# One-hot tiles of the gates: two tokens innermost instead of four

## The chip, the cores and the metric

The kernel runs on one core of one Trainium2 chip. The metric is the device time of one execution in microseconds. Before the change it is 1978.94 us, the median of three runs (1978.42 to 1980.65).

## The reference

The model has two layers over 256 tokens of width 1024. Layer 0 mixes with a gated linear attention beside an RWKV-7 scan, layer 1 with sparse attention. Behind each mixer stands a feed-forward part that picks 128 of 16384 experts for every token (8 heads of 16). The change lies in this part alone:

```python
q = (x @ w_q).reshape(B, T, PEER_HEADS, 2, PEER_DKEY // 2)
s = jnp.einsum('bthcd,hcnd->bthcn', q, sub_keys)
top_s, top_i = lax.top_k(s, PEER_TOPK)
cand_s = (top_s[..., 0, :, None] + top_s[..., 1, None, :]).reshape(B, T, PEER_HEADS, -1)
cand_i = (top_i[..., 0, :, None] * PEER_NKEYS + top_i[..., 1, None, :]).reshape(...)
best_s, pos = lax.top_k(cand_s, PEER_TOPK)
idx = jnp.take_along_axis(cand_i, pos, axis=-1)
gate = jax.nn.softmax(best_s, axis=-1)
h = gelu(einsum('md,mkd->mk', xb, exp_u[ib]))
coef = gate * h
out = einsum('mk,mkd->md', coef, exp_v[ib])
```

An expert's number is a pair of keys (a, b), each below 128, and its number is 128 a + b.

## The kernel before

The kernel gathers no experts. In `peer` it multiplies all tokens with all 16384 rows of u, 128 rows to a tile (128 tiles, L255 to L276, the u loop), and later with all rows of v (L283 to L308, the v loop). Between the two, every coefficient is multiplied by its gate, which is zero for experts that were not picked. The coefficients stand in two SBUF tiles, `Ca` and `Cb`: partition = second key, then the first key (72 of them in `Ca`, 56 in `Cb`), then the token.

A weight tile is read by one DMA of 512 KB on SP's queue (L86). ScalarE rounds it to a high part `wh` (L100), VectorE subtracts to get the low part `wl` (L101), and TensorE does three products of 256 columns for each of eight slices (L112 to L114 in the u loop, 24 matmuls a tile) or of 512 columns (L122 in the v loop, 12 matmuls a tile). ScalarE puts the Gelu of two u tiles into `Ca` or `Cb` (L264, L267).

The picks of a token come from `route`, which runs on VectorE during the first part of the u loop. It leaves the tile `picks`: 128 picks on the partitions, and for each of 256 tokens the first key, the second key and the gate as two f16 numbers (high and low part).

From this `gates` builds the gate matrix of four tokens at a time, 64 groups in a layer. `B` (`ohB`) is the one-hot code of the second key, `A` (`ohA`) that of the first key, multiplied by the two parts of the gate. Both come from a comparison of `iota` (0 to 127, every number repeated for each token) with `picks` (L318, L319), and `A` from two products in place (L321). Then TensorE adds, for each of the four tokens, two products of 128 columns: `B` of the token is the stationary operand, `A` of the token the moving one (L324, 8 matmuls a group). VectorE multiplies the result in PSUM into the coefficients that are already there (L330); where the u loop has not been yet, ScalarE copies it (L332) and the Gelu is multiplied in later (L268).

What sets the order: `peer` runs u tiles and pulls steps of the background work (`route`, then `gates`) by a budget of 1.65 a tile, a group of gates costing 2.1 (L246 to L276). A tile framework adds the waits, and it lets an instruction on an engine go ahead of others of the code where its operands are there early: the one-hots of the first groups run at 308 us, long before the first gate matmul. Behind that, one-hots are built about one group ahead of their matmuls. The pools that matter: `ohA` and `ohB` have two buffers each, `wh`, `wl` and `raw` three.

Of the kernel before, what the change touches and what calls it, by code (L numbers as in the profile page):

```python
# [15 lines left out]
F16 = mybir.dt.float16  # L16
AF = mybir.ActivationFunctionType
OP = mybir.AluOpType
# [3 lines left out]
P = 128  # L22
# [47 lines left out]
class Core:  # L70
# [63 lines left out]
    def consts(self):  # L134
        nc, a = self.nc, self.a
        c = self.const.tile([P, 3 * P + 16], F32, name="cst")
        nc.sync.dma_start(c, a["cst"])
        self.ident = c[:, 0:P]
        self.iota = self.const.tile([P, P, 4], F16, name="iota")
        nc.gpsimd.tensor_copy(self.iota, c[:, P:2 * P].unsqueeze(2).to_broadcast([P, P, 4]))  # L140
        self.ones = c[:, 2 * P:3 * P]
        self.iota16 = self.const.tile([P, 16, 16], BF16, name="iota16")
        nc.gpsimd.tensor_copy(self.iota16, c[:, 3 * P:3 * P + 16].unsqueeze(2).to_broadcast([P, 16, 16]))
        e = self.const.tile([P, 2], F32, name="eps")
        nc.vector.memset(e[:, 0:1], LN_EPS)
        nc.vector.memset(e[:, 1:2], LNX_EPS)
        self.eps = e
# [163 lines left out]
    def gates(self, pk, Ca, Cb, picks, t4, k):  # L311
        nc = self.nc
        V = nc.vector
        p = self.aps()
        B = pk.tile([P, P, 4], F16, name="ohB", bufs=2)
        A = pk.tile([P, 2, P, 4], F16, name="ohA", bufs=2)
        bc = lambda n: picks[:, n, t4:t4 + 4].unsqueeze(1).to_broadcast([P, P, 4])
        V.tensor_tensor(B, self.iota, bc(1), op=OP.is_equal)  # L318
        V.tensor_tensor(A[:, 1], self.iota, bc(0), op=OP.is_equal)  # L319
        for m in range(2):  # L320
            V.tensor_mul(A[:, m], A[:, 1], bc(2 + m))  # L321
        for n in range(4):
            for m in range(2):
                nc.tensor.matmul(p[:, n * P:(n + 1) * P], B[:, :, n], A[:, m, :, n], start=m == 0, stop=m == 1)  # L324
        g = p.rearrange("p (t i) -> p i t", t=4)
        for c, o, n in ((Ca, 0, CUT), (Cb, CUT, P - CUT)):
            c = c[:, :, t4:t4 + 4]
            q = min(max(k - o, 0), n)
            if q:
                V.scalar_tensor_tensor(c[:, :q], g[:, o:o + q], 1 / GATE, c[:, :q], op0=OP.mult, op1=OP.mult)  # L330
            if q < n:
                nc.scalar.activation(c[:, q:], g[:, o + q:o + n], AF.Copy, scale=1 / GATE)  # L332
# [677 lines left out]
    def blocks(self, pp, LbT, Tn, Tt):  # L1010
        nc = self.nc
        V, S = nc.vector, nc.scalar
        B, W = 16, P * (P + 1)
        DU = pp.tile([P, 2, B * B], F32, name="DU", tag="ths")
        D, U = (DU[:, n].rearrange("p (m j) -> p m j", m=B) for n in range(2))
        R = pp.tile([P, B * B], F32, name="R", tag="x4", bufs=4)
        nc.gpsimd.memset(U, 0.0)
# [124 lines left out]
```

## Time and profile before

| | |
|---|---|
| median of three runs | 1978.94 us |
| span of the profiled execution | 1976.5 us (the page gives this span as its only time; 2.4 us less than the median) |
| busy: TensorE matmul / VectorE / ScalarE | 97% / 71% / 47% of the span |
| first and last gate matmul, layer 0 | 376.0 and 667.0 us |
| first and last gate matmul, layer 1 | 1307.6 and 1598.7 us |
| gate matmuls (L324) | 1024, each with a weight load of its own |
| one-hot operations of VectorE (L318, L319, L321) | 512 |

Times are from the start of the span. The duration that the profile gives for a matmul or a weight load holds the latency of its pipeline, and neighbours overlap. What a matmul costs when many stand behind one another is read from the distance of their starts, or from the chain of waits, which cuts the time into pieces that don't overlap.

### The profile page before, as it was taken

The numbers are of one execution on the slowest core, as the hardware profiler recorded it, in microseconds if no ns is written. First come the engines' busy times: TensorE is split into PE (matmuls) and PEld (weight loads), VectorE is DVE, ScalarE is ACT, GpSimd is POOL, SyncE is SP. The second block draws the span as 40 slices with busy tenths as digits, with TensorE's granted clock in tenths as the row PEclk, the third lists the DMA queues.
The fourth block names the chain that finished last, engine by engine and source line by source line (L and its number), as shares of the span: only waits on it lengthen the run. The fifth ranks groups of instructions, "written<-read, shape, count | busy, mean of one in ns | idle before, by whom it ended". The sixth has DMA issues, their size and how long they took to land.

```text
span 1976.5 us, 32655 instructions
## 1 busy us (share of the span) xinstructions
PE 1926.1 (97%) x12834; PEld 1759.3 (89%) x12834; DVE 1404.4 (71%) x2860; ACT 932.7 (47%) x1385; POOL 20.8 (1%) x30
## 2 busy tenths in 40 slices
PE   8899899999999999999999989999999999999998
PEld 7898899999999988888888889999999998888886
DVE  6766599877788755556657959977788865555664
ACT  5435355544444444445534745544444444444552
POOL 1000000000000000000001100000000000000000
PEclk9999999999999999999999999999999999999999
DMA  7604345544444566667744445454444456666772
GB/s 225 187 33 130 117 150 161 175 146 148 141 149 146 159 191 191 192 192 232 230 151 150 128 136 173 151 162 148 148 142 147 141 170 192 192 192 195 234 230 76
DMA packets 96313, 323.83 MB, mean 164 GB/s; under 512 B 13984, under 2 KB 19360, under 8 KB 95264
## 3 DMA queue, kind: packets, MB, share of 16 engines
q1 hardware_dynamic: 96160, 321.76, 52.5%
q8 instruction: 100, 1.64, 0.3%
q14 instruction: 53, 0.43, 0.1%
HBM read 318.44 MB, written 3.28 MB: 163 GB/s over the span
## 4 chain that ended last, share of the span: by engine, by line
PE 80%; DVE 12%; DMA 5%; ACT 2%; issue 1%; SPq 0%; DVEq 0%; POOL 0%; ACTq 0%; POOLq 0%
PE acc L122 32%; PE wps L113 11%; PE wps L114 11%; PE wps L112 11%; PE acc L324 6%; DVE wl L101 4%; DMA raw<-v 4%; ACT wh L100 1%; PE acc L112 1%; PE acc L113 1%; PE acc L114 1%; DVE Cb L352 1%; PE wps L548 1%; PE wps L659 1%; PE wps L163 1%
## 5 line engine op out<-in xcount | busy, mean ns | idle before, releaser
L101 DVE TENSOR_TENSOR wl<-raw,wh 128x1024 fp32r<-128x1024 f32 x554 | 677.1, 1223 | 288.8 <-ACT wh L100 284.9
L100 ACT CAST wh<-raw 128x1024 fp32r<-128x1024 f32 x554 | 581.2, 1050 | 613.5 <-PE wps L113 266.3
L112 PE MATMUL wps<-xh,wh 128*128 128x256 f32 x2176 | 630.6, 290 | 0.3 <-ACT wh L100 0.2
L114 PE MATMUL wps<-xh,wl 128*128 128x256 f32 x2176 | 618.0, 284 | 9.9 <-DVE wl L101 9.9
L113 PE MATMUL wps<-xl,wh 128*128 128x256 f32 x2176 | 618.2, 284 | 0.0
L114 PEld LDWEIGHTS wps<-xh,wl 128*128 128x128 f32 x2176 | 419.7, 193 | 11.2 <-DVE wl L101 11.2
L112 PEld LDWEIGHTS wps<-xh,wh 128*128 128x128 f32 x2176 | 422.2, 194 | 1.5 <-ACT wh L100 0.7
L113 PEld LDWEIGHTS wps<-xl,wh 128*128 128x128 f32 x2176 | 420.7, 193 | 0.5 <-DVE xl L168 0.4
L122 PE MATMUL acc<-wh,cl 128*128 128x512 f32 x960 | 298.9, 393 | 0.0
L122 PE MATMUL acc<-wl,ch 128*128 128x512 f32 x960 | 298.1, 392 | 0.8 <-DVE wl L101 0.6
L122 PE MATMUL acc<-wh,ch 128*128 128x512 f32 x960 | 296.8, 390 | 0.0
L122 PEld LDWEIGHTS acc<-wh,ch 128*128 128x128 f32 x960 | 180.1, 188 | 40.9
L122 PEld LDWEIGHTS acc<-wl,ch 128*128 128x128 f32 x960 | 179.8, 188 | 41.0 <-DVE wl L101 3.2
L122 PEld LDWEIGHTS acc<-wh,cl 128*128 128x128 f32 x960 | 180.3, 188 | 39.0
L324 PE MATMUL acc<-ohA,ohB 128*128 128x128 f16 x1024 | 142.6, 296 | 0.0
L330 DVE SCALAR_TENSOR_TENSOR Ca<-acc,Ca 128x288 f32<-128x288 f32 (+12 forms) x128 | 55.2, 432 | 81.8 <-PE acc L324 81.4
L321 DVE TENSOR_TENSOR ohA<-ohA,picks 128x512 f16<-128x512 f16 x256 | 108.0, 422 | 5.4
L324 PEld LDWEIGHTS <-ohB 128*128 128x128 f16 x1024 | 103.8, 118 | 6.9
L112 PE MATMUL acc<-xh,wh 128*128 128x256 f32 x328 | 98.2, 300 | 2.4 <-ACT wh L100 2.4
L113 PE MATMUL acc<-xl,wh 128*128 128x256 f32 x328 | 95.0, 290 | 0.0
L114 PE MATMUL acc<-xh,wl 128*128 128x256 f32 x328 | 93.8, 288 | 0.8 <-DVE wl L101 0.8
L303 ACT CAST ch<-Ca 128x512 fp32r<-128x512 f32 x72 | 44.6, 622 | 83.8 <-PE acc L122 83.8
(397 smaller groups left out, 1747.4 us busy)
## 6 DMA issues: line engine op xcount, KB each, us to landing
raw<-u SPq DMA_DIRECT2D x256, 512.0 KB, 3.6
raw<-v SPq DMA_DIRECT2D x256, 512.0 KB, 4.2
raw<-win SPq DMA_DIRECT2D x41, 512.0 KB, 4.1
raw<-wout SPq DMA_DIRECT2D x16, 512.0 KB, 3.6
raw<-wq SPq DMA_DIRECT2D x16, 512.0 KB, 3.7
gb<-ln SPq DMA_DIRECT2D x2, 1024.0 KB, 5.9
Ca<-subk SPq DMA_DIRECT2D x2, 1024.0 KB, 4.9
Cb<-ln SPq DMA_DIRECT2D x2, 1024.0 KB, 6.8
```

What stands on the lines that cost most here:

```text
L100: self.nc.scalar.copy(h, raw)
L101: self.nc.vector.tensor_sub(l, raw, h.bitcast(F32))
L112: mm(out, h[:, s], xh[:, k], start=k == 0, stop=False)
L113: mm(out, h[:, s], xl[:, k], start=False, stop=False)
L114: mm(out, l[:, s], xh[:, k], start=False, stop=k == 7)
L122: mm(acc[tb * 2 + dh], x[:, c], y[:, dh * 512:(dh + 1) * 512], start=first and n == 0, stop=last and n == 2)
L163: nc.tensor.transpose(p[:, k * P:(k + 1) * P], self.x[:, tb, (g * 4 + k) * P:(g * 4 + k + 1) * P], self.ident)
L303: nc.scalar.copy(ch, C(i))
L321: V.tensor_mul(A[:, m], A[:, 1], bc(2 + m))
L324: nc.tensor.matmul(p[:, n * P:(n + 1) * P], B[:, :, n], A[:, m, :, n], start=m == 0, stop=m == 1)
L330: V.scalar_tensor_tensor(c[:, :q], g[:, o:o + q], 1 / GATE, c[:, :q], op0=OP.mult, op1=OP.mult)
L352: V.match_replace(s[:, g], tv[:, g, 0:8], s[:, g], MARK)
```

## The change

The tiles `ohB`, `ohA` and `iota` get another order in memory. Before, the innermost four elements are the same key of four tokens; a token's column is read with a step of four elements (8 bytes). Now the four tokens are two pairs, each pair has a block of 128 keys x 2 tokens of its own, and a token's column is read with a step of two elements (4 bytes). `iota` holds every number twice instead of four times, and both blocks read it. The operand of `picks` was four neighbouring elements repeated 128 times; now it is two neighbouring elements repeated 128 times, then the next two.

Every operation of VectorE has 512 elements a partition as before, every matmul 128 columns as before. The sequence of instructions and their waits is the same on every engine; only the copy that fills `iota` on GpSimd (L140) has 256 elements instead of 512. One line is added, so lines from L319 on stand one lower in the new kernel.

```diff
-        self.iota = self.const.tile([P, P, 4], F16, name="iota")
-        nc.gpsimd.tensor_copy(self.iota, c[:, P:2 * P].unsqueeze(2).to_broadcast([P, P, 4]))
+        self.iota = self.const.tile([P, P, 2], F16, name="iota")
+        nc.gpsimd.tensor_copy(self.iota, c[:, P:2 * P].unsqueeze(2).to_broadcast([P, P, 2]))
...
-        B = pk.tile([P, P, 4], F16, name="ohB", bufs=2)
-        A = pk.tile([P, 2, P, 4], F16, name="ohA", bufs=2)
-        bc = lambda n: picks[:, n, t4:t4 + 4].unsqueeze(1).to_broadcast([P, P, 4])
-        V.tensor_tensor(B, self.iota, bc(1), op=OP.is_equal)
-        V.tensor_tensor(A[:, 1], self.iota, bc(0), op=OP.is_equal)
+        B = pk.tile([P, 2, P, 2], F16, name="ohB", bufs=2)
+        A = pk.tile([P, 2, 2, P, 2], F16, name="ohA", bufs=2)
+        bc = lambda n: picks[:, n, t4:t4 + 4].rearrange("p (a b) -> p a b", a=2).unsqueeze(2).to_broadcast([P, 2, P, 2])
+        iota = self.iota.unsqueeze(1).to_broadcast([P, 2, P, 2])
+        V.tensor_tensor(B, iota, bc(1), op=OP.is_equal)
+        V.tensor_tensor(A[:, 1], iota, bc(0), op=OP.is_equal)
         for m in range(2):
             V.tensor_mul(A[:, m], A[:, 1], bc(2 + m))
         for n in range(4):
             for m in range(2):
-                nc.tensor.matmul(p[:, n * P:(n + 1) * P], B[:, :, n], A[:, m, :, n], start=m == 0, stop=m == 1)
+                nc.tensor.matmul(p[:, n * P:(n + 1) * P], B[:, n // 2, :, n % 2], A[:, m, n // 2, :, n % 2], start=m == 0, stop=m == 1)
```

## Rows read from the trace of the kernel before

**Rows 1.** The page: busy us, share of the span, instructions of each engine.
```profile
PE 1926.1 (97%) x12834; PEld 1759.3 (89%) x12834; DVE 1404.4 (71%) x2860; ACT 932.7 (47%) x1385; POOL 20.8 (1%) x30
```
**Rows 2.** The page: the chain that ended last, by engine.
```profile
PE 80%; DVE 12%; DMA 5%; ACT 2%; issue 1%; SPq 0%; DVEq 0%; POOL 0%; ACTq 0%; POOLq 0%
```
**Rows 3.** Stretches of the span: both gate stages, then the v loop.
```profile
core 0: us, PE busy (x) PEld busy (x) DVE busy (x) ACT busy (x) POOL busy (x), PEclk, DMA share, GB/s
376.00:667.00 291.00, 291.00 (x2433) 287.50 (x2432) 229.01 (x468) 127.86 (x247) 0.00 (x0) 1.00 0.47 146
1307.60:1598.70 291.10, 291.10 (x2434) 287.57 (x2433) 228.99 (x469) 127.91 (x247) 0.00 (x0) 1.00 0.48 146
667.00:1015.00 348.00, 347.69 (x1587) 287.57 (x1586) 208.78 (x203) 175.96 (x204) 0.00 (x0) 1.00 0.66 205
```
**Rows 4.** Chain of waits, layer 0's gate stage: by line, and a piece (start, us).
```profile
by line: PE wps L113 26.4%; PE wps L112 26.4%; PE wps L114 26.3%; PE acc L324 21.0%
...
441.27 0.96 PE acc L324 x8
```
**Rows 5.** Chain of waits elsewhere: a piece of the v loop, one of layer 0's mixer.
```profile
684.62 252.25 PE acc L122 x1102
134.41 0.75 PE wps L691 x13
```
**Rows 6.** Costliest groups of layer 0's gate stage: count, busy us, mean ns, idle before.
```profile
L112 PE MATMUL wps<-xh,wh 128*128 128x256 f32 x640 | 186.5, 291 | 0.0
L324 PE MATMUL acc<-ohA,ohB 128*128 128x128 f16 x511 | 71.2, 296 | 0.0
```
**Rows 7.** Weight loads by line: duration ns min/median/max, first and last start us, forms.
```profile
L324 PEld LDWEIGHTS <-ohB x1024: 111/117/138, 376.0 to 1598.6; 128*128 128x128 f16 x171
L112 PEld LDWEIGHTS wps<-xh,wh x2176: 186/192/338, 216.5 to 1615.6; 128*128 128x128 f32 x198
L691 PEld LDWEIGHTS wps<-Tn,Lb x32: 133/138/138, 134.0 to 137.9; 128*64 128x64 f32 x32
```
**Rows 8.** One-hot operations by line, same columns.
```profile
L318 DVE TENSOR_TENSOR ohB<-iota,picks x128: 412/416/427, 307.9 to 1591.7; 128x512 f16<-128x512 f16 x128
L319 DVE TENSOR_TENSOR ohA<-iota,picks x128: 415/418/426, 308.4 to 1592.9; 128x512 f16<-128x512 f16 x128
L321 DVE TENSOR_TENSOR ohA<-ohA,picks x256: 405/424/431, 308.9 to 1595.8; 128x512 f16<-128x512 f16 x128
```
**Rows 9.** Waits in layer 0's gate stage: us in total, times, longest us.
```profile
DVE Ca L330 <- PE acc L324: 39.1, 50, 1.6
...
DVE ohB L318 <- PE acc L324: 10.8, 11, 1.6
DVE wl L101 <- ACT wh L100: 7.5, 12, 0.8
```
**Rows 10.** Groups of VectorE outside the stage, shapes kept apart.
```profile
L1026 DVE TENSOR_TENSOR R<-DU 128x225 f32<-128x225 f32 x1 | 0.6, 550 | 0.0
...
L1026 DVE TENSOR_TENSOR R<-DU 128x144 f32<-128x144 f32 x1 | 0.4, 409 | 0.0
L999 DVE TENSOR_TENSOR wk<-wk,dcst 128x256 f32<-128x256 f32 x1 | 0.4, 425 | 0.0
L999 DVE TENSOR_TENSOR wk<-wk,dcst 128x128 f32<-128x128 f32 x1 | 0.3, 285 | 0.0
```
**Rows 11.** Further lines, by line.
```profile
L416 DVE TENSOR_TENSOR Cb<-Ca x2: 272/273/274, 284.6 to 1213.5; 128x128 f32<-128x128 f32 x2
L304 DVE TENSOR_TENSOR cl<-Cb,ch x52: 683/686/694, 877.1 to 1947.3; 128x512 fp32r<-128x512 f32 x52
L140 POOL CAST iota<-cst x1: 609/609/609, 4.2 to 4.2; 128x512 f16<-128x512 f32 x1
```

## The prediction

> **What bounds the kernel now.** I read the page's engine table first, then its chain, then the two stretches in which the gate matmuls run, and last the rows of single operations. The table shows TensorE busy for 97% of the span [rows 1]; since matmul durations overlap, this alone proves little. The chain, which has no overlaps, puts 80% of the span on TensorE and 12% on VectorE [rows 2]. [...] VectorE is early, not late: it waits for the gate matmuls for 39.1 us in front of L330 and 10.8 us in front of L318 [rows 9]. So a nanosecond taken from a gate matmul is a nanosecond of the stage, and one added to a one-hot operation is at first free.
>
> **What a gate matmul costs now.** 21.0% of 291 us is 61.1 us for 64 groups of 8: 119.3 ns each (one piece of the chain shows 0.96 us for a group of 8, which is 120 ns) [rows 4]. Set against it the other matmuls. L112 takes 26.4% of 291 us for 640 pieces [rows 4, 6]: 120.0 ns for 256 columns. L122 takes 252.25 us for 1102 pieces [rows 5]: 228.9 ns for 512 columns. The line through these two has a slope of 108.9/256 = 0.425 ns a column and an offset of 11.1 ns. For 128 columns it gives 65.5 ns. The gate matmul has 128 columns and takes 119.3 ns, which is 11.1 ns plus 128 columns at 0.845 ns: its columns come at half the rate. What differs is that L112 and L122 read 4-byte elements that lie next to each other, a step of 4 bytes from column to column, while L324 reads 2-byte elements with a step of 8 bytes. After the change the step is 4 bytes, so a column asks memory for no more than in L112.
>
> **The cost of each part.**
>
> Matmuls: 1024 of them, all on the path. The trace shows no 2-byte matmul with a step of 4 bytes, so I bound it. Lower end 65.5 ns, the line above. An upper end with the full column rate but with the weight load not hidden: the fp32 loads take 192 ns for 128 columns and 138 ns for 64 [rows 7], so 84 ns of a load are latency and 0.84 ns go to a column; the gate's load of 117 ns thus streams for 33 ns, and 65.5 + 33 = 98.5 ns. The outermost end is today's 119.3 ns. That it becomes slower I exclude: a smaller step with the same number of elements touches less memory, and the rows with that step are the fast ones. I take 70 ns, near the lower end, because L112 is the nearest row and hides weight loads that last longer. The term: 1024 x (119.3 - 70) = 50.5 us less; 55.1 and 21.3 us at the ends.
>
> One-hot operations: 512 on VectorE, 416 to 424 ns for 512 elements [rows 8]. An fp32 operation of that size takes 686 ns [rows 11], so today two elements go in a step. The change leaves 512 elements, 2-byte types and a step of one at the innermost place, so I keep the times. The bounds: 686 ns if the pairing is lost, and something between if repeating one 4-byte word 128 times is slow. For the latter, L1026 reads one operand in hops of single words: 409 ns for 144 elements and 550 ns for 225, 1.74 ns an element, against 1.09 for the contiguous L999 (285 ns for 128, 425 ns for 256) [rows 10]. That is 0.65 ns more for each word, 166 ns for 256 words, about 585 ns an operation. But L416 reads an operand in which one 4-byte word is repeated 16 times, and takes 273 ns for 128 elements [rows 11], no more than L999's 285 ns. The new operand repeats a word too and doesn't hop, so L416 is the nearer row and I take nothing. A gain below today's time is excluded on the same ground, since the operation keeps its 256 steps.
>
> The rest: the copy of `iota` on GpSimd is 609 ns at 4.2 us [rows 11], 300 us ahead of its first reader, and its cost is nothing either way. Nothing is moved and no wait is added.
>
> What is late next: each gate stage falls from 291 to about 291 - 25.2 = 265.8 us. VectorE's 229 us would then fill 86% of it, and the 25 us come out of the 49.9 us that it now waits for gate matmuls [rows 9]. ScalarE's 128 us and the DMA (146 GB/s over 291 us is 42.5 MB, which in 266 us is a rate of 160 GB/s; the v loop runs at 205) are further off [rows 3]. For tiles in which VectorE now has less time in hand I give back 1.2 us in each stage, an estimate, some 5% of the gain. The sum, against the profiled span of 1976.5 us: -50.5 + 2.4 = -48.1, so 1928.4 us; the median of the runs is 2.4 us above this span, which gives 1931 us.
>
> **The rivals.**
>
> *The matmuls stay at 119 ns.* For it: the gate's weight loads are recorded with 117 ns [rows 7], 2 ns below the distance of the matmuls, so the loads could set the pace, one latency after another. Then a smaller step brings at most the 6 ns from the median to the minimum of 111, 6 us in all, 1973 us, or nothing, 1979 us. Against it: L691's loads are recorded with 138 ns, and its matmuls follow each other after 0.75 us / 13 = 58 ns [rows 5, 7]; a load's recorded duration doesn't hold the next matmul back there.
> [...]
>
> *VectorE pays for single words.* At 585 ns an operation, 256 operations in a stage add 256 x 166 ns = 42.5 us to the 229 us: 271.5 us, above the 265.8 us that TensorE would need. With the waits that VectorE cannot avoid (7.5 us for L101 [rows 9] and a little) the stage takes about 280 us: 2 x 11 us of gain are left, 1957 us. For it speaks L1026, against it L416.
> [...] L416's 273 ns show that a repeated word escaped the penalty there.
>
> *Slower than before: VectorE loses the pairing.* At 686 ns an operation the stage's one-hots add 256 x 266 ns = 68 us: VectorE needs 297 us, more than the whole stage takes now. With some 10 us of waits the stage is 307 us, 16 us longer, and the kernel takes about 2011 us, whatever TensorE gains. The point from which this decides is a one-hot of 416 + (291 - 229)/256 us = 658 ns. Against it: the innermost place still holds two neighbouring 2-byte elements in every operand, so there are pairs to take. For it: a run of two is the shortest in which a pair can stand, and no row has one.
>
> **How the numbers follow.** Forecast (matmuls between 65.5 and 98.5 ns): 0.54, with a range of its own from 1924 to 1960 us. Matmuls unchanged: 0.23, between 1973 and 1979 us. Single words: 0.10, 1957 us. Pairing lost: 0.11, 2011 us. The remaining 0.02 is a gain of another size. A change within 0.2% (4 us) cannot be told from none. Faster: 0.54 + 0.10 + 0.02 and 0.03 of the unchanged case, where the loads give back more than 4 us: 0.69. Same: 0.19. Slower: 0.12, with 0.01 for the unchanged case with a little loss on VectorE. The range runs from 1921 us to 1981 us: it takes in the unchanged case and leaves out the lost pairing and some of the tails.
>
> **What would show it.** Right: the chain of the gate stages has pieces of 8 gate matmuls of 0.53 to 0.6 us instead of 0.96, the stages last about 267 us each, the one-hots stay at 416 to 424 ns, and VectorE's waits for L324 are about halved. Wrong in size: pieces of 0.75 us. The first rival: 0.96 us and 291 us again. The second: one-hots near 585 ns and TensorE waiting for VectorE between groups. The third: one-hots near 690 ns and stages above 300 us. Outside the two stages nothing should differ.

## The result, and the profile after

The changed kernel takes 1923.99 us (median of 4 runs, 1922.75 to 1925.53) against 1978.78 us before (now the median of four runs): 54.8 us less, a ratio of 0.9719 with a 95% interval of 0.9708 to 0.9730. The forecast was 1931 us. The runs of one kernel differ by less than 3 us here, so the change is faster beyond doubt.

The engine table and the chain of the changed kernel's page, as [rows 1, 2] for before:

```profile
PE 1872.6 (97%) x12834; PEld 1708.2 (89%) x12834; DVE 1404.7 (73%) x2860; ACT 931.0 (48%) x1385; POOL 20.7 (1%) x30
...
PE 77%; DVE 13%; DMA 6%; ACT 2%; issue 1%; SPq 0%; DVEq 0%; POOL 0%; ACTq 0%; POOLq 0%
```

TensorE's busy time fell by 53.5 us, VectorE's by nothing (1404.4 and 1404.7 us). Busy shares say little, though: TensorE is at 97% in both. The two gate stages and the v loop, in the columns of [rows 3]:

```profile
377.30:640.90 263.60, 263.60 (x2434) 260.90 (x2433) 229.14 (x468) 126.80 (x247) 0.00 (x0) 1.00 0.51 161
1281.85:1545.45 263.60, 263.60 (x2434) 260.92 (x2433) 229.06 (x468) 126.80 (x247) 0.00 (x0) 1.00 0.51 161
640.90:989.00 348.10, 347.69 (x1588) 287.44 (x1586) 209.07 (x203) 175.92 (x204) 0.00 (x0) 1.00 0.66 206
```

Each gate stage went from 291.0 to 263.6 us, 27.4 us less, and the v loop stayed as it was. Twice 27.4 is 54.8 us: the two stages hold the whole gain. VectorE has the same 229 us of work in them as before. The granted clock is 1.00 as before.

The chain in layer 0's gate stage by line, with its first pieces, as [rows 4]; below them the first row of gate matmuls in the kernel before and the piece behind it:

```profile
by line: PE wps L112 30.3%; PE wps L114 29.1%; PE wps L113 29.1%; PE acc L325 11.5%
```
```profile
377.35 0.12 PE wps L114
377.47 0.48 PE acc L325 x8
377.94 0.17 PE wps L112
378.12 0.12 PE wps L113
```
```profile
376.16 0.95 PE acc L324 x8
377.11 0.12 PE wps L112
```

Eight gate matmuls (now L325) take 0.48 us of the chain instead of 0.96. The reader should also see the next piece: the first fp32 product behind them takes 0.17 us and not 0.12, and for that reason L112 has a larger share than L113 and L114, where before all three had the same. The chain of the kernel before has no such tail.

The weight loads, matmuls and one-hot operations by line, as [rows 7, 8] (duration ns min/median/max):

```profile
L325 PEld LDWEIGHTS <-ohB x1024: 96/97/100, 377.3 to 1545.4; 128*128 128x128 f16 x171
```
```profile
L319 DVE TENSOR_TENSOR ohB<-iota,picks x128: 414/418/427, 307.9 to 1539.3; 128x512 f16<-128x512 f16 x128
```
```profile
L320 DVE TENSOR_TENSOR ohA<-iota,picks x128: 414/420/430, 308.4 to 1540.6; 128x512 f16<-128x512 f16 x128
```
```profile
L322 DVE TENSOR_TENSOR ohA<-ohA,picks x256: 404/424/428, 308.9 to 1543.0; 128x512 f16<-128x512 f16 x128
```

The one-hots have kept their times within 2 ns, and a weight load is recorded 20 ns shorter. VectorE's waits in the stage, as [rows 9]:

```profile
DVE Ca L331 <- PE acc L325: 16.3, 28, 1.2
DVE wl L101 <- ACT wh L100: 6.9, 12, 0.9
DVE ohB L319 <- PE acc L325: 5.9, 11, 1.2
```

It now waits 22.2 us for the gate matmuls where it waited 49.9 us. The 27.7 us that went are what the stage lost: VectorE's idle time paid for the gain.

For the comparisons below I also measured a row of gate matmuls by starts: from the start of the last fp32 product ahead of the row to the start of the second one behind it, less 2 x 120 ns, as the median over all 128 rows. Before this is 948 ns, after it is 525 ns. 128 x 423 ns = 54.1 us. The first row of the changed kernel, with starts in the first column (the chain's pieces run from end to end, so its times lie later): 377.95 - 377.19 us less 0.24 us is 0.52 us.

```profile
377.19 0.28 PE L114 MATMUL wps<-xh,wl 128*128 128x256 f32 x1
377.31 0.63 PE L325 MATMUL acc<-ohA,ohB 128*128 128x128 f16 x8
377.75 0.36 PE L112 MATMUL wps<-xh,wh 128*128 128x256 f32 x1
377.95 0.28 PE L113 MATMUL wps<-xl,wh 128*128 128x256 f32 x1
```

### The profile page after: what moved, and what is told of

Same layout as the page of the kernel before. It is cut to its first block, busy times and chain, and to the rows that moved or that the text cites. A ratio compares the mean times of both kernels' runs of the same rounds, so it can differ in the third digit from the quotient of the medians.

```text
span 1922.7 us, 32655 instructions
## 1 busy us (share of the span) xinstructions
PE 1872.6 (97%) x12834; PEld 1708.2 (89%) x12834; DVE 1404.7 (73%) x2860; ACT 931.0 (48%) x1385; POOL 20.7 (1%) x30
## 4 chain that ended last, share of the span: by engine, by line
PE 77%; DVE 13%; DMA 6%; ACT 2%; issue 1%; SPq 0%; DVEq 0%; POOL 0%; ACTq 0%; POOLq 0%
PE acc L122 32%; PE wps L112 12%; PE wps L114 11%; PE wps L113 11%; DVE wl L101 5%; DMA raw<-v 4%; PE acc L325 3%; ACT wh L100 2%; PE acc L112 1%; PE acc L113 1%; PE acc L114 1%; DVE Cb L353 1%; PE wps L549 1%; PE wps L660 1%; PE wps L163 1%
## 5 line engine op out<-in xcount | busy, mean ns | idle before, releaser
L112 PE MATMUL wps<-xh,wh 128*128 128x256 f32 x2176 | 630.0, 290 | 0.3
L114 PE MATMUL wps<-xh,wl 128*128 128x256 f32 x2176 | 619.3, 285 | 9.9 <-DVE wl L101 9.9
L113 PE MATMUL wps<-xl,wh 128*128 128x256 f32 x2176 | 618.6, 284 | 0.0
L114 PEld LDWEIGHTS wps<-xh,wl 128*128 128x128 f32 x2176 | 419.5, 193 | 11.1 <-DVE wl L101 11.1
L112 PEld LDWEIGHTS wps<-xh,wh 128*128 128x128 f32 x2176 | 420.4, 193 | 1.3 <-ACT wh L100 0.7
L113 PEld LDWEIGHTS wps<-xl,wh 128*128 128x128 f32 x2176 | 419.8, 193 | 0.5 <-DVE xl L168 0.4
L122 PE MATMUL acc<-wh,cl 128*128 128x512 f32 x960 | 299.0, 393 | 0.0
L122 PE MATMUL acc<-wl,ch 128*128 128x512 f32 x960 | 298.0, 392 | 0.8 <-DVE wl L101 0.6
L122 PE MATMUL acc<-wh,ch 128*128 128x512 f32 x960 | 297.0, 390 | 0.0
L122 PEld LDWEIGHTS acc<-wh,ch 128*128 128x128 f32 x960 | 180.1, 188 | 40.7
L122 PEld LDWEIGHTS acc<-wl,ch 128*128 128x128 f32 x960 | 179.9, 188 | 40.9 <-DVE wl L101 2.9
L122 PEld LDWEIGHTS acc<-wh,cl 128*128 128x128 f32 x960 | 180.4, 188 | 39.0
L112 PE MATMUL acc<-xh,wh 128*128 128x256 f32 x328 | 98.4, 301 | 2.4 <-ACT wh L100 2.2
L113 PE MATMUL acc<-xl,wh 128*128 128x256 f32 x328 | 95.2, 290 | 0.0
L114 PE MATMUL acc<-xh,wl 128*128 128x256 f32 x328 | 93.8, 288 | 0.8 <-DVE wl L101 0.8
L325 PE MATMUL acc<-ohA,ohB 128*128 128x128 f16 x1024 | 81.0, 220 | 0.0
L304 DVE TENSOR_TENSOR cl<-Ca,ch 128x512 fp32r<-128x512 f32 x72 | 49.7, 692 | 42.7 <-ACT ch L303 42.7
```

Source lines behind the costliest of these rows:

```text
L112: mm(out, h[:, s], xh[:, k], start=k == 0, stop=False)
L113: mm(out, h[:, s], xl[:, k], start=False, stop=False)
L114: mm(out, l[:, s], xh[:, k], start=False, stop=k == 7)
L122: mm(acc[tb * 2 + dh], x[:, c], y[:, dh * 512:(dh + 1) * 512], start=first and n == 0, stop=last and n == 2)
L304: V.tensor_sub(cl, C(i), ch.bitcast(F32))
L325: nc.tensor.matmul(p[:, n * P:(n + 1) * P], B[:, n // 2, :, n % 2], A[:, m, n // 2, :, n % 2], start=m == 0, stop=m == 1)
```

## The experiments

The theories at the start: M, the step of the moving operand `ohA` sets the distance of the gate matmuls; W, the step of the stationary operand `ohB` sets it through the weight load. Changes are shown against the changed kernel.

**e1, only the moving tile has pairs; e2, only the stationary one.** The core of e1's edit, and of e2's:

```diff
-        B = pk.tile([P, 2, P, 2], F16, name="ohB", bufs=2)
+        B = pk.tile([P, P, 4], F16, name="ohB", bufs=2)
...
+                nc.tensor.matmul(p[:, n * P:(n + 1) * P], B[:, :, n], A[:, m, n // 2, :, n % 2], start=m == 0, stop=m == 1)
```
```diff
-        A = pk.tile([P, 2, 2, P, 2], F16, name="ohA", bufs=2)
+        A = pk.tile([P, 2, P, 4], F16, name="ohA", bufs=2)
...
+                nc.tensor.matmul(p[:, n * P:(n + 1) * P], B[:, n // 2, :, n % 2], A[:, m, :, n], start=m == 0, stop=m == 1)
```

Expected of e1:

> Only the moving tile ohA has pairs of tokens innermost (step 4 bytes); the stationary tile ohB keeps four (step 8 bytes). Theory M, the step of the moving operand sets the pace: gate matmuls about 57 ns apart as with both changed, gate stages 263 to 264 us each, 1924 us. Theory W, the stationary operand's step sets it through the weight load: 119 ns, stages 291 us, 1979 us. Both together: something between.

Expected of e2:

> Only the stationary tile ohB has pairs innermost; the moving tile ohA keeps a step of 8 bytes. Theory M: gate matmuls 119 ns apart, stages 291 us, 1979 us. Theory W: 57 ns, 264 us, 1924 us. The recorded weight load tells besides whether its fall from 117 to 97 ns came from its own step (97 here under either theory) or from the matmul beside it (117 here).

Measured: e1 1930.96 us, ratio to the kernel before on the same chip 0.9743 (0.9727 to 0.9759); e2 1979.00 us, ratio 0.9986 (0.9977 to 0.9996). Layer 0's gate stage and a row of matmuls in the chain, e1 and then e2 (on that chip the kernel before had 1982.23 us):

```profile
378.90:644.10 265.20, 265.20 (x2435) 262.45 (x2433) 229.45 (x469) 127.27 (x247) 0.00 (x0) 1.00 0.51 160
...
435.14 0.51 PE acc L328 x8
...
L328 PEld LDWEIGHTS <-ohB x1024: 111/113/133, 378.9 to 1550.9; 128*128 128x128 f16 x171
```
```profile
379.10:668.70 289.60, 289.60 (x2434) 286.79 (x2433) 229.01 (x468) 127.70 (x247) 0.00 (x0) 1.00 0.47 146
...
379.25 0.94 PE acc L328 x8
...
L328 PEld LDWEIGHTS <-ohB x1024: 97/115/118, 379.1 to 1599.7; 128*128 128x128 f16 x171
```

Theory M holds. The moving tile alone brings 25.9 of the 27.4 us of a stage, the stationary one alone 1.5 us. The rows agree: 948 ns before, 928 ns with the stationary tile changed, 555 ns with the moving one, 525 ns with both. The recorded weight load follows both steps: 113 ns with its own step at 8 bytes beside fast matmuls, 115 ns with its own step at 4 bytes beside slow ones, 97 ns with both at 4 bytes. In e1, loads recorded with 113 ns stand beside matmuls that are 59 ns apart (median). So a load's recorded time does not set the distance here, and the 2 ns between the two before, on which the first rival rested, were a coincidence.

**e3 and e4, other steps of the moving operand.** e3 puts both parts and four tokens innermost, a step of 16 bytes; e4 leaves a gap, a step of 6 bytes:

```diff
-        A = pk.tile([P, 2, 2, P, 2], F16, name="ohA", bufs=2)
+        A = pk.tile([P, P, 2, 4], F16, name="ohA", bufs=2).rearrange("p i m t -> p m i t")
...
```
```diff
-        A = pk.tile([P, 2, 2, P, 2], F16, name="ohA", bufs=2)
+        A = pk.tile([P, 2, 2, P, 3], F16, name="ohA", bufs=2)[:, :, :, :, 0:2]
```

Expected of e3:

> ohB has pairs; in ohA both parts of four tokens stand innermost, so the moving column has a step of 16 bytes, without unused space. If the cost of a column grows with the step above 4 bytes: about 0.83 x 2 = 1.7 ns a column, some 215 to 235 ns a matmul, stages near 291 + 512 x 0.11 = 347 us, about 2090 us. If there are two rates only, full up to some step and half above: 119 ns, 291 us, 1979 us.

Expected of e4:

> As the changed kernel, but the pairs of ohA lie at a pitch of three elements with one unused, a step of 6 bytes. If the cost grows with the step above 4 bytes: 1.5 x 57 = 85 ns, stages 230.4 + 512 x 0.093 = 278 us, about 1952 us. Two rates with the border between 4 and 6 bytes: 119 ns and 1979 us; between 6 and 8 bytes: 57 ns and 1924 us. VectorE writes and reads single words with gaps: if the single-word price of 0.65 ns a word holds here, the products and comparisons into ohA take about 580 ns instead of 420, and VectorE has 229 + 31 us, below the stage in every case but the last.

Measured: e3 2094.97 us and stages of 346.7 us, e4 1953.16 us and stages of 276.0 us, in one run each. The stage, a row of matmuls in the chain and the operations into `ohA`, e3 and then e4 (with the piece behind the row):

```profile
379.80:726.50 346.70, 346.70 (x2434) 294.01 (x2433) 229.15 (x469) 128.70 (x249) 0.00 (x0) 1.00 0.40 123
...
379.99 1.83 PE acc L328 x8
...
L323 DVE TENSOR_TENSOR ohA<-iota,picks x128: 417/421/481, 310.9 to 1707.3; 128x512 f16<-128x512 f16 x128
...
L325 DVE TENSOR_TENSOR ohA<-ohA,picks x256: 410/426/430, 311.4 to 1711.1; 128x512 f16<-128x512 f16 x128
```
```profile
378.10:654.10 276.00, 276.00 (x2434) 273.27 (x2433) 253.77 (x468) 127.66 (x247) 0.00 (x0) 1.00 0.50 153
...
378.28 0.71 PE acc L325 x8
378.99 0.14 PE wps L112
...
L320 DVE TENSOR_TENSOR ohA<-iota,picks x128: 584/595/653, 308.6 to 1567.0; 128x512 f16<-128x512 f16 x128
...
L322 DVE TENSOR_TENSOR ohA<-ohA,picks x256: 576/602/618, 309.2 to 1569.7; 128x512 f16<-128x512 f16 x128
```

The distance of starts (median) is 58 ns at a step of 4 bytes, 88 ns at 6, 115 ns at 8 (e2) and 229 ns at 16: it grows in proportion to the step, by some 14.3 ns a byte from 4 to 16 bytes. So there are not just two rates. Why a wider step costs more is not shown: no run looks behind the step. e4 also has a price on VectorE: with single words and gaps between them the operations into `ohA` take 595 and 602 ns instead of 420 and 424, 0.69 ns for each of 256 words. Every second of these words also starts off a 4-byte boundary; the two causes were not tried apart. The stage hides it, since VectorE then has 254 of 276 us.

**e5 and e6, the tail behind a row.** In the changed kernel a row of eight costs 525 ns and its matmuls are 57 ns apart; 67 ns are left over, the tail. Theory T has it paid once a row, theory E as a part of every matmul. e5 puts two groups back to back, e6 leaves the gate's low part out:

```diff
-                for t4 in range(0, T, 4):
-                    self.gates(pk, Ca, Cb, picks, t4, state["k"])
-                    state["m"] = t4 + 4
-                    yield 2.1
+                for t4 in range(0, T, 8):
+                    for o in (0, 4):
+                        self.gates(pk, Ca, Cb, picks, t4 + o, state["k"])
+                    state["m"] = t4 + 8
+                    yield 4.2
```
```diff
-        for m in range(2):
-            V.tensor_mul(A[:, m], A[:, 1], bc(2 + m))
+        V.tensor_mul(A[:, 0], A[:, 1], bc(2))
...
-            for m in range(2):
...
+            nc.tensor.matmul(p[:, n * P:(n + 1) * P], B[:, n // 2, :, n % 2], A[:, 0, n // 2, :, n % 2], start=True, stop=True)
```

Expected of e5:

> As the changed kernel, but two groups of gates stand back to back, 16 gate matmuls in a row, every second time. In the changed kernel a group takes 0.518 us of the stage (263.6 us less 230.4 us for 80 weight tiles, by 64), of which 8 x 57 ns are matmuls and some 60 ns lie behind the last one, on the next fp32 product. Theory T, this tail is paid once per row of gate matmuls because the fp32 weight load behind it is hidden by a 57 ns matmul alone: 32 tails fewer, stages 261.7 us, 1920 us or 0.2% below the changed kernel. Theory E, every gate matmul costs 65 ns wherever it stands: 263.6 us and 1924 us. If VectorE is not ready for two groups at a time, TensorE waits between groups and the stage is longer.

Expected of e6:

> As the changed kernel, with the low part of the gate left out: one product on VectorE and four gate matmuls a group fewer. Theory T (8 x 57 ns and a tail of 60 ns a group): a group takes 0.289 us, stages 248.9 us. Theory E (65 ns each): 0.259 us, stages 247.0 us. The time falls to about 1894 or 1890 us if TensorE still bounds the stage; VectorE needs about 202 us.

Measured: e5 1923.84 us, ratio 0.9703 (0.9688 to 0.9718); e6 1900.17 us in one run, stages of 248.2 us. A row in the chain, e5 and then e6:

```profile
378.95 0.94 PE acc L326 x16
```
```profile
379.02 0.25 PE acc L323 x4
```

By starts a row of 4, 8 and 16 costs 296, 525 and 983 ns: 57.2 ns for each matmul and 67 ns once a row. That is theory T. Not all of the 67 ns lies behind the row: the first two gate matmuls are 71 ns apart and not 57 (14 ns), the first starts 122 and not 120 ns after the fp32 product ahead (2 ns), and from the start of the last one to the start of the second fp32 product behind it 228 ns pass, 51 more than 57 + 120 (medians).

What these 51 ns are made of was not tried by itself. An estimate: fp32 weight loads take 192 ns for 128 columns and 138 ns for 64 [rows 7], 0.84 ns a column or 107 ns for 128 columns; if only the last 57 ns matmul lies over them, 50 ns are left. Runs with slower matmuls bear it out in the main. The same distance is 228 ns behind a 57 ns matmul and 232 ns behind an 88 ns one (e4): up to there the gate matmul does not set it, as if a load of fixed length did, and 24 ns are left in e4 where the estimate has 19. Behind a 115 ns matmul (e2) it is 250 ns; the 15 ns that are left there are not explained by it.

e6's total was expected at 1894 us and was 6 us above; on its chip the kernel before took 1981.73 us, 3 us more than in the first timing. Its stages came out as expected.

e5's stage, read from the first to the last gate matmul, is 258.8 us, 4.8 us less than with single groups, but that overstates it: the last row is a pair, so fewer weight tiles lie between the first and the last matmul. From the first gate matmul to the start of the v loop it is 279.0 us against 281.0 us. The total was no clear gain against the first timing (0.9703 and 0.9719, with intervals that overlap), so the two were also timed side by side on one chip.

**e8 and e9, the changed kernel and the two groups again, side by side.** The kernels are those of the change and of e5.

Expected of e8:

> The changed kernel once more, beside the version with two groups back to back on the same chip: 1924 us or a ratio of 0.972 to the kernel before, and the 525 ns of TensorE's stage for a row of eight gate matmuls as in its first profile.

Expected of e9:

> Two groups back to back, on the same chip as the changed kernel. A row of 4, 8 and 16 gate matmuls has cost the stage 296, 525 and 983 ns so far: 57.2 ns each and 67 ns once a row. Theory T: 32 tails fewer in each layer, 2 x 2.1 us, so 4 us or 0.2% below the changed kernel. If the waits of VectorE take this back, no difference between the two.

Measured: e8 1924.30 us, ratio 0.9733 (0.9720 to 0.9746); e9 1919.51 us, ratio 0.9701 (0.9688 to 0.9715). By the medians two groups back to back are 4.8 us faster than the change alone, by the means 4.1 us, where theory T had 4. The totals alone carry this only just: the intervals miss each other by 0.0005, and the runs overlap (1917.74 to 1926.67 us and 1917.51 to 1922.43 us). The stage is clearer: from the first gate matmul to the v loop it is 280.96 us in each layer for e8 and 279.04 us for e9, 3.8 us less over the two layers, as between the change and e5 before. The gate stage of e8's profile,

```profile
372.90:636.50 263.60, 263.60 (x2435) 260.89 (x2433) 229.16 (x468) 126.93 (x247) 0.00 (x0) 1.00 0.50 161
```

is the same 263.6 us, though this profile's span is 1915.6 us, 7 us shorter than the first. Most of the difference lies ahead of the first gate matmul (372.9 and 377.3 us) and in the mixer of layer 1, which the change doesn't touch: the stage is a sharper measure than the total.

**e7, one token innermost.**

```diff
...
-        A = pk.tile([P, 2, 2, P, 2], F16, name="ohA", bufs=2)
-        bc = lambda n: picks[:, n, t4:t4 + 4].rearrange("p (a b) -> p a b", a=2).unsqueeze(2).to_broadcast([P, 2, P, 2])
+        A = pk.tile([P, 2, 4, P], F16, name="ohA", bufs=2)
+        bc = lambda n: picks[:, n, t4:t4 + 4].unsqueeze(2).to_broadcast([P, 4, P])
...
```

Expected of e7:

> One token innermost: each token has its own block of 128 keys, a column is read with a step of 2 bytes, and the operand of picks is one 2-byte element repeated 128 times. If the pairing of VectorE is lost (third rival of the prediction): one-hots at about 686 ns, VectorE 297 us in a stage, stages 300 to 310 us, about 2000 to 2011 us, and TensorE waits for the one-hots. If a repeated element keeps the pairing: 420 ns and 1924 us. The gate matmuls stay at 57 ns if 128 columns at the full rate are their floor, and fall if the pace follows the step below 4 bytes too.

Measured: 1974.60 us in one run, stages of 288.2 and 288.9 us. The products by line, then the stage, then who waits:

```profile
L322 DVE TENSOR_TENSOR ohA<-ohA,picks x256: 673/684/706, 309.1 to 1594.9; 128x512 f16<-128x512 f16 x128
...
378.00:666.20 288.20, 274.03 (x2446) 264.89 (x2445) 283.42 (x470) 127.73 (x249) 0.00 (x0) 0.99 0.48 145
...
PE wps L114 <- DVE wl L101: 11.6, 16, 0.9
```

The pairing is lost, at 684 ns as the prediction's third rival had priced it, and VectorE bounds the stage. Its total was a miss: 1974.6 us instead of 2000 to 2011. I had added 266 ns for each of 256 operations to 229 us, 297 us; VectorE was busy for 283 us, and it had 5 us of idle time left and not 10. The step that failed was to add recorded durations to a busy time. Summed, VectorE's durations in the stage do rise by 65 us, from 255 to 320 us (248 of the operations start in it). But neighbours overlap in the records, by 26 us in the changed kernel and by 37 us here, and busy time counts an overlap once: 54 us are left. The matmuls of a row are 56 ns apart at a step of 2 bytes and 58 ns at 4 (medians): below 4 bytes next to nothing more is gained.

## Why the prediction was right

**The bound.** "A nanosecond taken from a gate matmul is a nanosecond of the stage" held, with a chain of TensorE alone in layer 0's stage before [rows 4] and after: 54.1 us fewer by rows, 54.8 us fewer in the stages and in the total.

**The cause.** The half rate of the columns came from the moving operand's step, as the comparison with L112 and L122 [rows 4 to 6] had it; e1 and e2 show it, and e3 and e4 show that the cost grows with the step. Steps of 8 and 6 bytes are not free for 2-byte columns: a matmul takes 115 ns (e2) and 88 ns (e4) against 58 ns at 4 bytes.

**The size of the term.** I took 70 ns a matmul, between 65.5 and 98.5. Their distance is 57 ns, below my lower end, and close to the 54.4 ns of the line's slope alone: the line's offset of 11.1 ns does not carry over to gate matmuls, for a reason that no run shows. In exchange there are the 67 ns once a row, which I had not seen. The two make 525/8 = 65.6 ns, by luck the lower end. So the term was 54 us and not 50.5.

**What I gave back.** The 2.4 us for VectorE did not come: its chain share in the stages is nil, and its waits for the gate matmuls fell from 49.9 to 22.2 us, a little more than the half I had named. The 3.6 us by which the term was too small and these 2.4 us are what the forecast (48 us less) missed of the measured 54.8 us, but for 0.7 us.

**The rivals.** Matmuls unchanged: no. Single words: the one-hots stayed at 418 to 424 ns. These times confirm that L416 [rows 11] and not L1026 [rows 10] was the nearer row; in e4, words with gaps do cost 0.69 ns each (L1026 had 0.65). A gap alone does not cost that: e3's operations into 8-byte runs at a pitch of 16 bytes keep 421 and 426 ns. Nor does a word that is repeated in place, as the operand of `picks` now has it. Pairing lost: not with two tokens, but with one (e7), where a stage is 25 us longer than in the changed kernel. My price for it was too high: I had 16 us more than before for each stage, and e7's stages are 2 to 3 us shorter than before, since VectorE's overlapping durations added less than their sum.

## What to carry to other kernels

Compare the distance of matmul starts per column with that of another matmul in the same trace; where it is longer, look at the step of the moving operand before the weights (here it brought 25.9 us of a stage, the stationary one 1.5). Choose the innermost count by both readers: of one, two and four, two is here the smallest that leaves VectorE its pairs (a product takes 424 ns, with one 684) and the largest that gives TensorE its full rate (58 ns a matmul, with one 56, with four 115). Then ask what lies behind the row that became faster: here 67 ns were paid once a row, so longer rows pay them less often; that a long weight load behind a short matmul is the cause is an estimate that e4 and e2 agree with in the main; no run tested it alone.

## What the hardware showed that I had not expected

A 2-byte moving operand of 128 columns takes 56, 58, 88, 115 and 229 ns at steps of 2, 4, 6, 8 and 16 bytes (granted clock 0.99 to 1.00): flat up to 4 bytes, then in proportion to the step. The step of the stationary operand matters little: 8 to 4 bytes saves 20 to 30 ns in a row of eight. And a row of f16 matmuls in front of fp32 products costs 67 ns more than its matmuls, whether it has 4, 8 or 16 of them (at a step of 4 bytes).
